# The gMLP layer's u and z as seven products of 2x2 blocks in place of eight

## The chip, the cores and the metric

One NeuronCore of a Trainium2 chip runs the whole step. The metric is the device time of one execution in microseconds. A NeuronCore has a matrix engine (TensorE, PE in the profile), a vector engine (VectorE, DVE), an engine for functions and copies (ScalarE, ACT), a general engine (GpSimd, POOL) and one whose instructions issue most DMAs (SyncE, SP). Each runs its own instruction stream in the order in which it was written, and semaphores join them.

## What is computed

The reference is one step of a model of two layers, over 512 prompt and 128 sample tokens (640 columns or five token tiles of 128). Layer 0 is a Mamba-2 mixer, which the change leaves as it was. Layer 1 is a gMLP:

```python
proj = h @ w_in                         # 1024 -> 3 x 2048
u = gelu(proj[..., :G_WIDTH])
v = gelu(proj[..., G_WIDTH:2 * G_WIDTH])
z = proj[..., 2 * G_WIDTH:]
v = layer_norm(v, ln_w, ln_b)
s = W_s @ v + b                         # 128x128 position matrix per group, 8 groups
y = u * s * silu(z)
out = y @ w_out                         # 2048 -> 1024, added to the residual
```

and a last RMS norm follows. All of it is float32. Each float32 product is made of three passes in TensorE's reduced format: operands are split in a high part (a rounding cast) and a low part (what is left), and high x high, high x low and low x high are summed.

## The kernel before

`Stream` (lines 103 to 136) brings weight blocks of 128x1024 from DRAM, two blocks ahead; `wsplit` casts the high part on ACT (L99) and subtracts it on DVE (L100) for the low part. `mm` (L69) is every matrix product.

Layer 1 has three stages. **v**: `v_tile` makes four blocks `vb` of 512 features for five token tiles `t`, 24 products of 512 columns each. Through block 0, the transposes of the normed input (`hT`, high and low; ACT L230, DVE L231) for tile t+1 are put in the middle of tile t. The weights of the next block are cast while tile 4 of a block runs. A GELU (ACT L756) and statistics follow each tile, and in block 3 the normalization (DVE L763). The mixing matrices `spt` are loaded whole (L773), and their row sums `pr` (L736) made in this stage.

**u and z**: a loop over 16 feature tiles f (eight groups g, two tiles each). Per f, `in_proj` makes u and then z: 8 blocks of the input x 3 passes x two halves (384 and 256 columns), so 96 products. Five products with `spt` (`sp`, `sq`) mix the positions of v. GELU, tanh and DVE products give y, which `split` takes apart (ACT L294, DVE L295). The output projection of group g-1 (`out_proj`, 60 products of 512 columns, added to the residual by `accB`, DVE L801) stands between the two f of group g, for g from 1 to 6. In groups 0 to 3, POOL multiplies and adds a 256-column piece of v (L834, L835) for an output.

**The end**: behind f=15 the last two output projections stand one after the other; the last one's pieces go into `final`, the last norm.

PE's stream is in the written order. On the other engines a scheduler sets the order at build time, and it is then fixed.

Of the kernel before, what the change touches and what calls it, by code (L numbers as in the profile page):

```python
# [27 lines left out]
# columns of the packed small constants  # L28
_C = {}
_off = 0  # L30
for _n, _w in (("nw0", 8), ("ident", 128), ("dtb", 32), ("alog", 32), ("sel", 32), ("blk", 8),
               ("triP", 128), ("triS", 128), ("sufP", 128), ("sufS", 128),
               ("convw", 128), ("convb", 32), ("dskip", 16), ("anw", 16), ("lnw", 16), ("lnb", 16)):
    _C[_n] = (_off, _off + _w)
    _off += _w
NCST = _off
NCST1 = _C["triP"][0]      # loaded first
# [3 lines left out]
def hybrid_step(ctx: ExitStack, tc: tile.TileContext, xin, xT0, cst, wdt, cache, wA, wAo, h0in, wB, wBv, wBo,  # L41
# [4 lines left out]
    # ------------------------------------------------------------ shared pools  # L46
# [10 lines left out]
    csb = const.tile([P, NCST], F32, name="csb")  # L57
    ones = const.tile([P, P], F32, name="ones")
    V.memset(ones, 1.0)
    S.activation(small.tile([P, 1], F32, name="pre"), ones[:, 0:1], AF.Exp)      # loads the function table  # L60

    def C(n):
        a, b = _C[n]
        return csb[:, a:b]

    ident, triP, triS = C("ident"), C("triP"), C("triS")

    def mm(out, lhsT, rhs, start=True, stop=True):
        T.matmul(out, lhsT=lhsT, rhs=rhs, start=start, stop=stop)  # L69
# [36 lines left out]
    class Stream:  # L106
# [8 lines left out]
        # the first weights, in pieces  # L115
# [26 lines left out]
    # feature-major input times the norm weight, in H/L, and with it the projections to dt and to the first  # L142
    # feature tile; the norm's factor of each token (rs; on every partition: rb) is applied to the projections
    def norm_first(zp, rb):
        xH, xL = norm_tiles()
        xt = zp.tile([P, KD, NT], F32, name="xt")
        nc.sync.dma_start(out=csb[:, :8], in_=cst[:, :8])
# [7 lines left out]
        nc.sync.dma_start(out=csb[:, 8:NCST1], in_=cst[:, 8:NCST1])  # L155
# [12 lines left out]
        def dt_step(k):          # rows 0-31 with the high parts of the weights, rows 32-63 with the low ones  # L168
# [52 lines left out]
    # its transpose, feature-major, in H/L  # L221
# [11 lines left out]
    # feature tile of an input projection: W[:, tile].T @ x.T, in two column halves  # L233
# [8 lines left out]
    # column sums of [feature, token], tokens to partitions: [token, tile]  # L242
# [9 lines left out]
    side = deque()            # pieces of other work to put between the steps  # L252
# [16 lines left out]
    # token-major output projection of two feature tiles, added to h1  # L269
# [47 lines left out]
    for g in range(GROUPS):  # L317
        units += [(wB[f],) for f in (2 * g, 16 + 2 * g)]
        if 0 < g < GROUPS - 1:
            units += [(wBo[f],) for f in (2 * g - 2, 2 * g - 1)]  # L320
        units += [(wB[f],) for f in (2 * g + 1, 17 + 2 * g)]
    units += [(wBo[f],) for f in (12, 13, 14, 15)]
# [3 lines left out]
    # ============================================================ layer 0: SSD mixer  # L326
    with ExitStack() as ca:
# [5 lines left out]
        rb = ap.tile([P, NT], F32, name="rb")  # L333
        xT, px0, rs, norm_fin, norm_half = norm_first(pp, rb)
# [5 lines left out]
        nc.sync.dma_start(out=csb[:, NCST1:], in_=cst[:, NCST1:])  # L340

        cw = ap.tile([P, 160], F32, name="cw")        # half the conv weights and biases
        V.tensor_scalar(cw, csb[:, _C["convw"][0]:_C["convb"][1]], 0.5, None, ALU.mult)
# [3 lines left out]
        # ---------------- dt, decays (token-major [token, tile, head])  # L347
# [23 lines left out]
        # cumulative sums within each chunk (128 tokens of the prompt, 16 of a stream)  # L371
# [3 lines left out]
        # chunk totals, on every partition: 4 prompt chunks, then 8 streams  # L375
# [4 lines left out]
        # la and its exponential with heads on partitions, in DRAM, from where a head's row goes to all partitions  # L380
# [68 lines left out]
        for g in range(GROUPS):  # L449
# [14 lines left out]
            # x, B, C of the group; x and B also token-major  # L464
# [22 lines left out]
            # sample tokens in high and low parts; by way of DRAM, the parts of the 16 tokens of a stream come  # L487
            # one below the other, so that one pass gives all four products of a state's update
# [22 lines left out]
            # decays from each token to each later one of its chunk  # L511
# [45 lines left out]
            # ---- prompt states  # L557
# [16 lines left out]
            # ---- sample states, decayed, and what they give to y  # L574
# [18 lines left out]
            # ---- C B^T, masked  # L593
# [36 lines left out]
            # ---- y, by pairs of heads  # L630
# [30 lines left out]
            # ---- new sample states  # L661
# [11 lines left out]
            # ---- gate: g2 = 2 y silu(z); the factor 2 is taken back in the group norm  # L673
# [53 lines left out]
    # ============================================================ layer 1: gMLP mixer  # L727
    with ExitStack() as cb_:
        bp = cb_.enter_context(tc.tile_pool(name="bp", bufs=1))
        hT = hH, hL = norm_tiles()  # L730
        rsb = bp.tile([P, 8, 2, P], F32, name="rsb")

        # row sums of the mixing matrices, on every partition
        def row_sums(q, g4):
            pr = ps_m.tile([P, 4, P], F32, name="pr", tag="m")
            mm(pr, ones, spt[:, q, 4 * g4:4 * g4 + 4, :])  # L736
            S.copy(out=rsb[:, 4 * g4:4 * g4 + 4, q, :], in_=pr)

        # ---- v, token-major
        v = bp.tile([P, TT, 4, 512], F32, name="v", tag="v")  # L740
        st6 = bp.tile([P, TT, 4, 6], F32, name="st6")

        def v_tile(Wv, vb, t, mid=lambda: None):
            tsl = slice(t * P, (t + 1) * P)
            ps = bank("oomm"[(vb * TT + t) % 4], "pv")
            for k in range(KD):
# [7 lines left out]
                if t == 4 and k % 2:  # L754
                    stream.fill(k // 2 + 1)
# [9 lines left out]
        cv = ExitStack()  # L765
        rpool = cv.enter_context(tc.tile_pool(name="rpool", bufs=2))
        stream.pools.update({stream.n + i: rpool for i in range(16) if i % 4 > 1})
        with tc.tile_pool(name="xsp", bufs=1) as xsp:
# [3 lines left out]
            spt = bp.tile([P, 2, 8, P], F32, name="spt")     # prompt W^T, sample W^T  # L772
            nc.sync.dma_start(out=spt, in_=spc)  # L773
            bsb = bp.tile([P, 8, 2, P], F32, name="bsb")     # prompt b, sample b
            nc.sync.dma_start(out=bsb, in_=bsp)
# [176 lines left out]
```

## Time and profile before

| | us |
|---|---|
| median of 3 runs | 1116.09 |
| lowest, highest | 1112.14, 1117.57 |
| span of the profiled execution | 1111.9 |
| PE busy | 1057.9 (95%) |
| DVE busy | 786.4 (71%) |
| ACT busy | 393.7 (35%) |
| POOL busy | 212.0 (19%) |

The span is that of one execution under the profiler, from its first to its last instruction; it stands 0.24 us under the lowest run and 4.2 us under the median. Busy shares are means over all stages; layer 1's stages have to be read one by one.

### The profile page before, as it was taken

To read this page: it belongs to the slowest core of one execution; us is meant where nothing else is said; L and a number is where in the kernel's file an instruction comes from. 1 tells how busy PE (TensorE), PEld (TensorE's weight loads), DVE (VectorE), ACT (ScalarE), POOL (GpSimd) and SP (SyncE) were. 2 spreads that over 40 slices of the span, in tenths; PEclk is the share of its full clock that TensorE was granted. 3 is DMA by queue.
4 is the path that set the end of the run, shared out by engine and by line. 5 is a ranking of instruction groups with operands and counts; after the bars stand their busy time and mean duration, and the time that the engine had idled before them with its cause. 6 is when DMAs were issued, how large, how long until landed. Compare 5 with 4: busy or idle time off the path is not lost. (4 is left out here: it accounts for less than half of the span.)

```text
span 1111.9 us, 16826 instructions
## 1 busy us (share of the span) xinstructions
PE 1057.9 (95%) x6571; PEld 957.8 (86%) x6571; DVE 786.4 (71%) x1351; ACT 393.7 (35%) x691; POOL 212.0 (19%) x290
## 2 busy tenths in 40 slices
PE   8998999998998999989999999999999999999994
PEld 7897888798898897988997788889999999999983
DVE  7969887878879879798789942386545645545357
ACT  6363516226254162352542432222132122222214
POOL 3444322404214234052132000002200000000004
PEclk9898999999999999999999999999999999999997
DMA  7453435243362352523632522113332122221202
GB/s 250 138 182 113 162 94 174 83 157 121 95 206 85 98 179 89 187 85 94 206 97 97 224 76 76 48 59 122 109 101 76 57 85 69 76 74 54 82 19 95
DMA packets 50560, 124.89 MB, mean 112 GB/s; under 512 B 8593, under 2 KB 21137, under 8 KB 50225
## 3 DMA queue, kind: packets, MB, share of 16 engines
q1 hardware_dynamic: 50480, 123.81, 34.5%
q8 instruction: 52, 0.85, 0.3%
q14 instruction: 28, 0.22, 0.1%
HBM read 106.93 MB, written 16.86 MB: 111 GB/s over the span
## 5 line engine op out<-in xcount | busy, mean ns | idle before, releaser
L69 PE MATMUL pin<-xH,wh 128*128 128x256 f32 (+1 forms) x1280 | 409.3, 320 | 10.9 <-DVE xp L416 10.2
L69 PE MATMUL pin<-xH,wl 128*128 128x256 f32 (+1 forms) x1280 | 398.2, 311 | 0.5 <-DVE wl L100 0.5
L69 PE MATMUL pin<-xL,wh 128*128 128x256 f32 (+1 forms) x1280 | 398.2, 311 | 0.0
L69 PEld LDWEIGHTS pin<-xH,wh 128*128 128x128 f32 x1280 | 244.5, 191 | 19.6 <-ACT xc L432 11.2
L69 PEld LDWEIGHTS pin<-xL,wh 128*128 128x128 f32 x1280 | 245.0, 191 | 0.7 <-issue 0.3
L69 PEld LDWEIGHTS pin<-xH,wl 128*128 128x128 f32 x1280 | 244.6, 191 | 0.8 <-DVE wl L100 0.8
L99 ACT CAST wh<-raw 128x1024 fp32r<-128x1024 f32 x127 | 132.2, 1046 | 236.5 <-PE pin L69 127.2
L69 PE MATMUL pop<-wh,yHL 128*128 128x512 f32 x640 | 205.4, 402 | 5.8 <-DVE hs L570 5.1
L100 DVE TENSOR_TENSOR wl<-raw,wh 128x1024 fp32r<-128x1024 f32 x104 | 130.3, 1257 | 64.3 <-ACT wh L99 63.0
L69 PEld LDWEIGHTS pop<-wh,yHL 128*128 128x128 f32 x640 | 117.3, 188 | 36.4 <-DVE hs L570 7.8
L426 DVE SCALAR_TENSOR_TENSOR acc<-xp,cw,acc 128x664 f32<-128x664 f32 x96 | 114.4, 1192 | 17.9 <-ACT acc L423 16.6
L69 PE MATMUL pop<-wl,yHL 128*128 128x512 f32 x320 | 126.4, 395 | 0.0
L69 PEld LDWEIGHTS pop<-wl,yHL 128*128 128x128 f32 x320 | 60.1, 188 | 14.3
L801 DVE SCALAR_TENSOR_TENSOR h<-pop,h 128x512 f32<-128x512 f32 x80 | 53.7, 687 | 25.1 <-PE pop L69 24.2
L690 DVE SCALAR_TENSOR_TENSOR h<-pop,rr,h 128x512 f32<-128x512 f32 x80 | 59.0, 745 | 13.3 <-PE pop L69 13.2
L849 POOL TENSOR_TENSOR h<-h,fnw_sb 128x512 f32<-128x512 f32 x10 | 12.9, 1285 | 287.1 <-ACT oo L848 286.7
L69 PE MATMUL pv<-wh,xH 128*128 128x512 f32 x160 | 63.5, 397 | 0.0
L69 PE MATMUL pv<-wh,xL 128*128 128x512 f32 x160 | 62.4, 390 | 0.4 <-DVE xL L231 0.4
L69 PE MATMUL pv<-wl,xH 128*128 128x512 f32 x160 | 62.3, 389 | 0.0
L100 POOL TENSOR_TENSOR wl<-raw,wh 128x1024 fp32r<-128x1024 f32 x23 | 56.0, 2437 | 12.3 <-ACT wh L99 12.3
L519 ACT ACTIVATE E<-E,la 128x128 f32<-128x128 f32 x160 | 51.5, 390 | 17.1 <-DMA E<-laD 17.1
L432 ACT ACTIVATE xc<-acc 128x512 f32<-128x512 f32 x64 | 26.6, 463 | 71.2 <-DVE acc L426 71.2
(176 smaller groups left out, 1234.0 us busy)
## 6 DMA issues: line engine op xcount, KB each, us to landing
raw<-wA SPq DMA_DIRECT2D x47, 512.0 KB, 3.8
raw<-wB SPq DMA_DIRECT2D x32, 512.0 KB, 3.6
E<-laD SPq DMA_DIRECT2D x32, 320.0 KB, 6.4
h<-h0in SPq DMA_DIRECT2D x16, 512.0 KB, 4.5
raw<-wAo SPq DMA_DIRECT2D x16, 512.0 KB, 3.8
out_sspS<-h SPq DMA_DIRECT2D x16, 512.0 KB, 3.8
raw<-wBv SPq DMA_DIRECT2D x16, 512.0 KB, 4.6
raw<-wBo SPq DMA_DIRECT2D x16, 512.0 KB, 3.9
```

What stands on the lines that cost most here:

```text
L69: T.matmul(out, lhsT=lhsT, rhs=rhs, start=start, stop=stop)
L99: S.copy(out=H, in_=raw)
L100: eng.tensor_tensor(out=L, in0=raw, in1=H.bitcast(F32), op=ALU.subtract)
L426: V.scalar_tensor_tensor(acc[:, 0:664], xp[:, k:k + 664], cw[:, 4 * ft + k:4 * ft + k + 1], acc[:, 0:664], ALU.mult, ALU.add)
L432: S.activation(o, a, AF.Tanh)
L519: S.activation(E_[:, t, :], E_[:, t, :], AF.Relu, bias=la[:, t, h:h + 1], scale=-1.0)
L690: V.scalar_tensor_tensor(h1[:, t, dsl], ps, rg[:, t:t + 1], h1[:, t, dsl], ALU.mult, ALU.add)
L801: V.scalar_tensor_tensor(h1[:, t, dsl], ps, 0.5, h1[:, t, dsl], ALU.mult, ALU.add)
L849: G.tensor_tensor(out=h1[:, t, dsl], in0=h1[:, t, dsl], in1=fnw_sb[:, dsl], op=ALU.mult)
```

## The change

u and z of one feature tile are seen as a 2x2 block product: the rows of the left matrix are u's and z's weights, its columns the two halves of the 1024 input features (blocks a11, a12, a21, a22 of 128x512), and the right matrix's blocks are the input's feature halves x token halves of 320 columns. Seven products m1 to m7 of summed blocks, in Winograd's form of Strassen's scheme, take the place of the eight.

- `Forms` loads u's and z's raw block, adds and subtracts 512-column pieces on POOL (L758, L760, L761, L765), and splits each of seven pieces (ACT L744, DVE L745). Pieces of the output weights go the same way, unsummed.
- The input's summed blocks are made once, from high and low parts, in ten POOL instructions of 1280 columns written into block 1 of v (`t1_`, `t2_`, `t34_`; L848, L851); each sum is split (ACT L854, DVE L855) into `tf`, the fourth (t3) over block (0,1) of the input after the last tile of v.
- `prod` is 12 products of 320 columns; seven of them make 84 per f. PSUM sums of products are joined by ACT copies (L953, L958), DVE adds (L955, L963, L965, L974) and one POOL add (L959).
- `position` loads the mixing matrices per group, in a pool that takes over the space of the summing stage; `pr`, of 256 columns, opens each group.
- The output projection of group g-1 stands before the second f in every group from 1 to 7. Behind the loop only the last one is left.

```diff
+        def split(self, src):
+            t = wpool.tile([P, 2, 512], F32R, name="wf", tag="wh" if len(self.got) % 2 == 0 else "wl", bufs=4)
+            S.copy(out=t[:, 0], in_=src)
+            V.tensor_tensor(out=t[:, 1], in0=src, in1=t[:, 0].bitcast(F32), op=ALU.subtract)
+            self.got.append(t)
...
+            def first():
+                G.tensor_tensor(out=t1, in0=a21, in1=a22, op=ALU.add)
+                self.split(a11)
+                G.tensor_tensor(out=a21, in0=a11, in1=a21, op=ALU.subtract)
+                G.tensor_tensor(out=a11, in0=t1, in1=a11, op=ALU.subtract)
+            def a12_():
+                self.split(a12)
+                G.tensor_tensor(out=a12, in0=a12, in1=a11, op=ALU.subtract)
+            return [first, lambda: self.split(a11), lambda: self.split(t1), a12_, lambda: self.split(a21),
+                    lambda: self.split(a12), lambda: self.split(a22)]
...
+            def t1_():
+                sub(ta, f12[0], f11[0])
+                sub(tx, f12[1], f11[1])
+                add(ta, ta, tx)
+                hilo(ta, tf[:, 0, 0], tf[:, 0, 1])
...
+                    if vb == 1 and t in (0, 2, 4):
+                        (t1_, t2_, t34_)[t // 2]()
+            hilo(t3, *block(0, 1))
...
+        def position(g):
+            spt = wk.tile([P, 2, P], F32, name="spt", tag="spt", bufs=2)
+            nc.sync.dma_start(out=spt, in_=spc[:, :, g, :])
+            G.memset(spt[64:128, 0, 0:64], 0.0)
...
-                if i and 0 < g < GROUPS - 1:
-                    out_proj([stream.next(), stream.next()], prev, accB, banks="oommoommoo")
+                if i and g:
+                    Ws = out_weights()
+                    for p in range(2 * TT):
+                        out_piece(Ws, prev, p)
...
+                prod(pa, "m1", True)
+                S.copy(out=c1, in_=pa)
+                prod(pb, "m6", True)
+                V.tensor_tensor(out=uu[:, hi], in0=pb, in1=c1, op=ALU.add)
+                pc = ps_m.tile([P, 512], F32, name="pqc", tag="m")[:, :HT]
+                prod(pc, "m5", True)
+                S.copy(out=c5, in_=pc)
+                G.tensor_tensor(out=c5, in0=c1, in1=c5, op=ALU.add)
+                prod(pa, "m2", False)
+                S.activation(uu[:, lo], pa, AF.Gelu)
+                prod(pb, "m7", False)
+                V.tensor_tensor(out=zz[:, hi], in0=pb, in1=c5, op=ALU.add)
+                prod(pc, "m3", False)
...
+                prod(pb, "m4", False)
+                V.tensor_tensor(out=zz[:, lo], in0=pb, in1=c1, op=ALU.add)
```

Three places in the instruction order. The first is ACT where block 1 of v begins (`v<-pv` is a GELU, `wh` a weight cast, `tf` the cast of a summed input block). Before:

```order
L756 ACTIVATE v_6395<-pv_6647 128x512
L99 CAST wh_6697<-raw_6695 128x1024
L99 CAST wh_6709<-raw_6707 128x1024
L99 CAST wh_6721<-raw_6719 128x1024
L99 CAST wh_6733<-raw_6731 128x1024
L756 ACTIVATE v_6395<-pv_6688 128x512
L756 ACTIVATE v_6395<-pv_6740 128x512
```

After:

```order
L819 ACTIVATE v_6395<-pv_6632 128x512
L99 CAST wh_6682<-raw_6680 128x1024
L854 CAST tf_6397<-tx0_6728 128x1280
L99 CAST wh_6694<-raw_6692 128x1024
L99 CAST wh_6706<-raw_6704 128x1024
L854 CAST tf_6397<-tx1_6729 128x1280
L99 CAST wh_6718<-raw_6716 128x1024
L819 ACTIVATE v_6395<-pv_6673 128x512
L854 CAST tf_6397<-tx0_6728 128x1280
L819 ACTIVATE v_6395<-pv_6732 128x512
```

and POOL there, which had no instruction at this place before:

```order
L848 TENSOR_TENSOR tx0_6728<-xH_6393 128x1280
L848 TENSOR_TENSOR tx3_6731<-xL_6394 128x1280
L848 TENSOR_TENSOR tx2_6730<-xH_6393 128x1280
L851 TENSOR_TENSOR tx0_6728<-tx0_6728,tx3_6731 128x1280
L848 TENSOR_TENSOR tx1_6729<-xH_6393,tx0_6728 128x1280
L848 TENSOR_TENSOR tx3_6731<-xL_6394 128x1280
L851 TENSOR_TENSOR tx1_6729<-tx1_6729,xL_6394 128x1280
L851 TENSOR_TENSOR tx2_6730<-tx2_6730,tx3_6731 128x1280
L848 TENSOR_TENSOR tx0_6728<-xH_6393,tx1_6729 128x1280
L851 TENSOR_TENSOR tx0_6728<-tx0_6728,xL_6394 128x1280
```

The casts of block 1's weights now have casts of summed inputs between them, the first behind POOL's fourth instruction and the second behind its seventh.

The second is PE at the end of v (`pv`), before:

```order
L69 MATMUL pv_7244<-wh_7058,xL_6393 128x512
L69 MATMUL pv_7244<-wl_7059,xH_6392 128x512
L69 MATMUL pin_7318<-xH_6392,wh_7253 128x384
L69 MATMUL pin_7318<-xL_6393,wh_7253 128x384
L69 MATMUL pin_7318<-xH_6392,wl_7254 128x384
```

After:

```order
L69 MATMUL pv_7246<-wh_7060,xL_6394 128x512
L69 MATMUL pv_7246<-wl_7061,xH_6393 128x512
L69 MATMUL pr_7343<-spt_7338,ones_83 128x256
L69 MATMUL pqa_7354<-xH_6393,wf_7259 128x320
L69 MATMUL pqa_7354<-xL_6394,wf_7259 128x320
```

and DVE there (`wf` is a split of a weight piece; the row of `xL` makes the low part of t3):

```order
L745 TENSOR_TENSOR wf_7289<-raw_7253,wf_7289 128x512
L745 TENSOR_TENSOR wf_7298<-raw_7255,wf_7298 128x512
L745 TENSOR_TENSOR wf_7307<-raw_7301,wf_7307 128x512
L820 BN_STATS st6_6396<-v_6395 128x6
L855 TENSOR_TENSOR xL_6394<-tx2_6730,xH_6393 128x4x320
```

The first product of the u and z stage was one with streamed weights; now it is `pr`, whose `spt` is loaded into space that the summing stage gives up with DVE's `xL<-tx2`.

The third is PE behind the last f. Before:

```order
L69 MATMUL sp_10073<-spt_6417,v_6395 128x128 x4
L69 MATMUL sq_10074<-spt_6417,v_6395 128x128
L69 MATMUL pop_10103<-wh_9955,yHL_9583 128x512 x2
L69 MATMUL pop_10103<-wl_9956,yHL_9583 128x512
L69 MATMUL pop_10103<-wh_10014,yHL_9812 128x512 x2
```

After:

```order
L69 MATMUL sp_10461<-spt_9701,v_6395 128x128 x4
L69 MATMUL sq_10462<-spt_9701,v_6395 128x128
L69 MATMUL pqb_10351<-tf_6397,wf_10391 128x320 x12
L69 MATMUL pop_10500<-wf_10412,yHL_10248 128x512 x3
L69 MATMUL pop_10500<-wf_10444,yHL_10494 128x512 x3
L69 MATMUL pop_10510<-wf_10428,yHL_10248 128x512 x3
L69 MATMUL pop_10510<-wf_10468,yHL_10494 128x512 x3
```

Before, the last but one output projection (60 products on group 6's y) follows `sq`, and the first product on the last f's y is the 64th behind it; now it is the fourth behind the last `m4` (`yHL_10494` is the last f's y).

## Rows read from the trace of the kernel before

**Rows 1.** Stages of layer 1 (windows): length, then busy us by engine, PEclk, DMA.
```profile
658.00:742.50 84.50, 84.50 (x371) 69.07 (x370) 38.38 (x80) 22.12 (x29) 0.00 (x0) 1.00 0.20 66
742.50:1070.60 328.10, 328.10 (x2061) 311.64 (x2060) 171.81 (x249) 83.01 (x126) 15.08 (x16) 1.00 0.26 83
1070.60:1111.90 41.30, 27.26 (x117) 21.60 (x115) 30.61 (x72) 14.03 (x30) 12.85 (x10) 0.87 0.17 64
```

**Rows 2.** Chain of waits, pieces in order of time: start us, us, what.
```profile
742.64 14.09 PE pin L69 x96
...
788.26 13.99 PE pop L69 x60
...
1069.87 18.20 PE pop L69 x78
```

**Rows 3.** Timeline of PE where v ends: start us, us, instruction.
```profile
742.25 0.39 PE L69 MATMUL pv<-wl,xH 128*128 128x512 f32 x1
742.48 0.33 PE L69 MATMUL pin<-xH,wh 128*128 128x384 f32 x1
```

**Rows 4.** Lines by form, PE: busy us, mean ns, idle before.
```profile
L69 PE MATMUL pr<-spt,ones 128*128 128x512 f32 x8 | 3.9, 592 | 0.0
```

**Rows 5.** Timeline of ACT around the second block of v.
```profile
650.57 1.08 ACT L230 CAST xH<-pt 128x512 fp32r<-128x512 f32 x2 [2.56 <-PE pt L228]
...
654.89 1.06 ACT L99 CAST wh<-raw 128x1024 fp32r<-128x1024 f32 x1 [0.54 <-PE pv L69]
```

**Rows 6.** Timeline of PE, first tile of the second block of v.
```profile
659.00 0.39 PE L69 MATMUL pv<-wh,xH 128*128 128x512 f32 x1
...
663.53 0.39 PE L69 MATMUL pv<-wl,xH 128*128 128x512 f32 x1
```

**Rows 7.** Lines by form, POOL.
```profile
L100 POOL TENSOR_TENSOR wl<-raw,wh 128x1024 fp32r<-128x1024 f32 x23 | 56.0, 2437 | 12.3 <-ACT wh L99 12.3
...
L849 POOL TENSOR_TENSOR h<-h,fnw_sb 128x512 f32<-128x512 f32 x10 | 12.9, 1285 | 287.1 <-ACT oo L848 286.7
```

**Rows 8.** Lines by form, ACT and DVE: the weight split.
```profile
L99 ACT CAST wh<-raw 128x1024 fp32r<-128x1024 f32 x127 | 132.2, 1046 | 236.5 <-PE pin L69 127.2 <-PE pop L69 85.2 <-DMA raw<-wA 6.4
...
L100 DVE TENSOR_TENSOR wl<-raw,wh 128x1024 fp32r<-128x1024 f32 x104 | 130.3, 1257 | 64.3 <-ACT wh L99 63.0
```

**Rows 9.** Timelines of POOL, then of DVE: additions and splits, side by side and alone.
```profile
758.78 0.74 POOL L834 TENSOR_TENSOR lwb<-v,lwb 128x256 f32<-128x256 f32 x1 [6.09 <-DMA lwb<-lnwb]
759.60 1.20 POOL L835 TENSOR_TENSOR lwb<-lwb 128x256 f32<-128x256 f32 x1
...
760.12 1.75 DVE L100 TENSOR_TENSOR wl<-raw,wh 128x1024 fp32r<-128x1024 f32 x1
...
1071.67 1.22 DVE L100 TENSOR_TENSOR wl<-raw,wh 128x1024 fp32r<-128x1024 f32 x1
```

**Rows 10.** Windows around PE's longest wait (2.9 us).
```profile
100.00:104.00 4.00, 2.74 (x11) 2.23 (x11) 3.84 (x9) 3.69 (x8) 0.40 (x2) 0.59 0.38 125
104.00:108.00 4.00, 4.00 (x28) 3.44 (x28) 3.02 (x3) 0.94 (x2) 2.35 (x1) 0.56 0.53 165
```

**Rows 11.** DMA issues: count, KB each, median us to landing.
```profile
out_sspP<-hs SPq DMA_DIRECT2D x8, 128.0 KB, 1.7
...
dw<-wdt SPq DMA_DIRECT2D x1, 128.0 KB, 3.0
```

**Rows 12.** Timelines of DVE, then of ACT, behind the last mixing product.
```profile
1070.35 0.41 DVE L816 SCALAR_TENSOR_TENSOR thb<-thb,pin 128x256 f32<-128x256 f32 x1
...
1070.94 0.82 DVE L817 TENSOR_TENSOR uu<-uu,thb 128x640 f32<-128x640 f32 x1
...
1072.81 0.82 DVE L838 TENSOR_TENSOR uu<-uu,sb 128x640 f32<-128x640 f32 x1
...
1074.74 0.82 DVE L295 TENSOR_TENSOR yHL<-uu,yHL 128x640 fp32r<-128x640 f32 x1
...
1073.71 0.73 ACT L294 CAST yHL<-uu 128x640 fp32r<-128x640 f32 x1 [3.72 <-DVE uu L838]
```

More of the change, by code (lines that the diff above doesn't have):

```diff
@@ L725, in hybrid_step, with __init__, raw, start @@
     out_proj([stream.next(), stream.next()], *pend.pop(GROUPS - 1))
+    class Forms:
+        def __init__(self, items, pool):
+            self.items, self.pool, self.got, self.n = items, pool, [], 0
+        def raw(self, src, i):
+            r = (self.pool if i else wpool).tile([P, 1024], F32, name="raw", tag="raw", bufs=2)
+            nc.sync.dma_start(out=r, in_=src)
+            return r
+        def split(self, src):
[3 more added lines that the diff above has]
+            self.got.append(t)
+        def start(self):
+            kind, s0, s1 = self.items.pop(0)
+            r0, r1 = self.raw(s0, 0), self.raw(s1, 1)
+            a11, a12, a21, a22 = r0[:, :512], r0[:, 512:], r1[:, :512], r1[:, 512:]
+            if kind == "o":
+                return [lambda x=x: self.split(x) for x in (a11, a12, a21, a22)]
+            t1 = self.pool.tile([P, 512], F32, name="s1", tag="s1", bufs=1)
+            def first():
[8 more added lines that the diff above has]
+                    lambda: self.split(a12), lambda: self.split(a22)]
+        todo = []
+        def fill(self, ahead):
+            while len(self.got) < self.n + ahead and (self.items or self.todo):
+                if not self.todo:
+                    self.todo = self.start()
+                self.todo.pop(0)()
+        def next(self, ahead):
+            self.fill(1 + ahead)
+            r = self.got[self.n]
+            self.got[self.n] = None
+            self.n += 1
+            return r[:, 0], r[:, 1]
     with ExitStack() as cb_:
@@ L730, in hybrid_step, with block @@
         hT = hH, hL = norm_tiles()
[L731 to L737, printed above, removed]
+        HT = NT // 2
+        def block(k, j):
+            ks, js = slice(4 * k, 4 * k + 4), slice(HT * j, HT * j + HT)
+            return hH[:, ks, js], hL[:, ks, js]
         v = bp.tile([P, TT, 4, 512], F32, name="v", tag="v")
         st6 = bp.tile([P, TT, 4, 6], F32, name="st6")
+        forms = Forms([x for g in range(GROUPS) for x in
+                       [("q", wB[2 * g], wB[16 + 2 * g])]
+                       + ([("o", wBo[2 * g - 2], wBo[2 * g - 1])] if g else [])
+                       + [("q", wB[2 * g + 1], wB[17 + 2 * g])]]
+                      + [("o", wBo[14], wBo[15])], bp)
         def v_tile(Wv, vb, t, mid=lambda: None):
@@ new lines, in hybrid_step, with prod @@
+        wk = cb_.enter_context(tc.tile_pool(name="wkb", bufs=2))
+        X = dict(m1=block(0, 0), m2=block(1, 0), m3=block(1, 1), m7=block(0, 1))
+        X |= {m: (tf[:, i, 0], tf[:, i, 1]) for i, m in enumerate(("m5", "m6", "m4"))}
+        def prod(ps, m, start, ahead=4):
+            wH, wL = forms.next(ahead)
+            xH, xL = X[m]
+            for k in range(4):
+                ks = slice(k * P, (k + 1) * P)
+                mm(ps, wH[:, ks], xH[:, k], start=(start and k == 0), stop=False, skip_group_check=not start)
+                mm(ps, wH[:, ks], xL[:, k], start=False, stop=False, skip_group_check=not start)
+                mm(ps, wL[:, ks], xH[:, k], start=False, stop=(k == 3), skip_group_check=not start)
@@ L800, in accB, with out_weights, out_piece @@
         def accB(ps, t, dsl):
             V.scalar_tensor_tensor(h1[:, t, dsl], ps, 0.5, h1[:, t, dsl], ALU.mult, ALU.add)
+        def out_weights():
+            w = [forms.next(3) for _ in range(4)]
+            return w[:2], w[2:]
+        def out_piece(Ws, ys, p, after=None):
+            t, dh = p // 2, p % 2
+            tsl, dsl = slice(t * P, (t + 1) * P), slice(dh * 512, (dh + 1) * 512)
+            ps = bank("oommoommoo"[p], "pop")
+            for i in range(2):
+                (wH, wL), (yH, yL) = Ws[i][dh], ys[i]
+                mm(ps, yH[:, tsl], wH, start=(i == 0), stop=False)
+                mm(ps, yL[:, tsl], wH, start=False, stop=False)
+                mm(ps, yH[:, tsl], wL, start=False, stop=(i == 1))
+            accB(ps, t, dsl)
+            if after is not None:
+                after(t, dsl, dh)
```

133 lines of the change are left out of this document (79 added, 54 removed).

## Prediction

> **What bounds the kernel now.** I read the stages of layer 1 first [rows 1]. In the u and z stage (742.5 to 1070.6 us) PE is busy for all of 328.1 us at full clock, while DVE works 171.8, ACT 83.0 and POOL 15.1 us of it: only fewer product columns shorten this stage, and there is room on the other engines on average. In v (658 to 742.5) PE is busy throughout and POOL does nothing. The last stage is mixed: PE 27.26 of 41.3 us. The chain of waits then shows what the stage is made of [rows 2]: per feature tile f one piece of 96 products in 14.09 us, and 13.99 us per output projection; the last piece, 78 products in 18.20 us, shows that the chain behind the last f is hidden under the last but one output projection. Last I look at where stages meet: the last product of v starts at 742.25 and the first of u at 742.48 [rows 3], no gap.
>
> **Part 1, the products.** The halves of 384 and 256 columns have a mean of 320, which is the new width, so 14.09 us / 96 = 0.1468 us is the price of a product of 320 columns by the mean of its two neighbours. Per f 84 products take the place of 96, an eighth less: 14.09 / 8 = 1.76 us, by 16 f **-28.2 us**. Output projections and mixing products stay. `pr` had eight products of 512 columns, 3.9 us [rows 4], and gets the same columns in eight of 256 and twice the places: 0.
>
> **Part 2, the input sums, at block 1 of v.** PE comes to this block at 659.00 and to the product that needs the low part of the fourth weight block at 663.53 [rows 6]. The four weight casts began at 654.89 [rows 5]. Now two casts of sums stand between them on ACT, and wait for POOL. POOL's first subtraction can start when the first half of the last token tile is cast, 650.57 + 0.54 = about 651.1 [rows 5]. Its price: 1285 ns for 512 columns and 2437 for 1024 [rows 7] make 1152 per 512, so 1280 columns are 2437 + 576 = 3.01 us. The first sum is ready after four of them (663.2), the second after seven (672.2). ACT: the cast of a sum is 1046 x 1280/1024 = 1.3 us at most [rows 8]; the second ends at 673.5, and the fourth weight cast, queued behind it, at 674.5. DVE: low part of the sum 1257 x 1.25 = 1.6 us [rows 8], to 675.1, then the weight's, 1.26: 676.3. So PE stands 676.3 - 663.5 = **12.8 us** if nothing else slows POOL.
> But it will be slowed. Where a POOL addition and a DVE split lie side by side, POOL's goes from 0.74 to 1.20 us and DVE's from 1.22 to 1.75 [rows 9]. About 5.4 us of such DVE work lies beside POOL before the second sum (three weights, 3.8, and one sum, 1.6), and 0.46 us per 1.22 of it makes 2.0 us; the two DVE steps at the end, 2.9 us, stretch by up to 0.53/1.22, 1.2 us. Sum 16.0: I take **+16**, with ends 12.8 (no meeting) and 20 (the stretch twice as large).
> The Trainium skill says, in "GPSIMD Engine Reference", Key points, that POOL shares its SBUF interfaces with DVE and contends with DVE instructions that have two SBUF inputs, and that elementwise work is about twice as fast on DVE. The two rows bear it out; without such sharing this term would be 12.8 and my sum 3.2 us lower, and the rule speaks against the ten additions' place.
> Then the clock. Around a wait of 2.9 us the granted clock was 0.59 and 0.56 in two windows of 4 us [rows 10], between the levels 2.4 and 1.2 GHz; of full speed that loses 0.41 x 2.74 + 0.44 x 4.00 = 2.9 us, of which part can lie in the wait. I take **+2** for this wait, ends 0 and 3.
>
> **Part 3, where v ends.** PE's first instruction is now `pr`; it waits for POOL's memset of `spt`, that for the load, and that for DVE's low part of t3, which frees the space. Count from T, the end of v. Weight pieces wait for slots that v's last products free, so POOL's sum for the next f, its a21 and this f's a12 (three of 1.285 us [rows 7], the first begun some 1.4 us ahead of T) end at T+2.5. Behind them ACT casts three pieces of about 0.57 us (half of 1046 and a little) and a GELU of 0.6: T+4.8. DVE is then at the last pieces' low parts and statistics (0.7 each), T+6.2, and does t3's low part, 1.6: about T+7.7. The load of 128 KB lands in 1.7 to 3.0 us [rows 11]: T+9.4 to T+10.7. I take **+10.5** for PE's wait, ends 8.5 (no split late) and 13 (POOL and DVE stretched as in part 2), and for the clock behind it again **+2**, ends 0 and 3. Behind `pr` the weights' pieces are ready.
>
> **Part 4, the end.** Behind the last `m4` come an add of 320 columns (about 0.48, between 0.41 for 256 columns and the 0.82 of 640), tanh (0.73 by the cast of the same width), four DVE steps at 0.82 and one cast of 0.73 [rows 12]: 0.48 + 0.73 + 3.28 + 0.73 = 5.2 us, with handovers 5.6. Only three products of 512 columns (0.23 each [rows 3]) stand between: **+4.9**, ends 3.5 (some hidden) and 7 (weight splits queued between on DVE). The clock behind it: +0.5, ends 0 and 1.5, since DVE sets the pace of the last norm anyway. The output projection that was the cover (13.99) is only moved to an earlier place.
>
> **Part 5, u and z otherwise.** Per f, DVE gets seven half splits for two whole ones (4.4 for 2.5 us), four adds of about 0.48 and a whole-width step for two halves (0.82 for 0.97): +3.6 us, by 16 58, so 230 of 300 us. POOL gets four additions of 1.285 and one of about 0.9: 6.0 us per f. What covers it is that pieces are made four ahead; handovers: **+2**, ends 0 and 6. The loads of `spt` go out one group ahead; a group's some 40 us of products hide their 3 us, and without that cover each of seven would cost what part 3 has.
>
> **Sum**: -28.2 + 16 + 2 + 10.5 + 2 + 4.9 + 0.5 + 2 = **+9.7 us**. The sum stands on the profiled execution, 1111.9 us of span, 0.24 under the lowest run; the median is 1116.09, 4.2 above that span. Put on the median: **1125.8 us**. Ends of all terms together: -3.4 and +25.3.
>
> **Rivals.**
> *No held casts* (faster). If POOL's first seven instructions were done before PE needs the casts (some 659, so 1.1 us each), part 2 falls away: 9.7 - 18 = -8.3, 1107.8 us. For it speaks only that no row shows 1280 columns on POOL; against it the two sizes that rows 7 show. If ACT could pass a waiting cast it would come out the same way. The Trainium skill ("TensorE: Matmul & The Clock Gate", Engine queue depths) says ACT and DVE queues are strictly in order; no row here shows an ACT instruction passing another. Chance 0.13.
> *Early mixing matrices* (no change). If t3's low part is done beside v's last products, `spt` lands as v ends and part 3 falls away: 9.7 - 12.5 = -2.8, 1113.3 us. Against it: t3 is written over a block that v's last products still read. Chance 0.12.
> *DVE becomes the bound* (slower still). POOL's new 6.0 us per f are 96 us; if each stretched DVE by as much as itself, DVE would have 230 + 96 = 326 us in a stage of 300: +26 less the 2 above, 1149 us; it decides from 70/96 = 0.73 us of stretch per us of POOL on. Rows 9 give 0.53 us for an addition of 0.74 alone, 0.72, if every one of them met a split of two inputs from SBUF; DVE's reads from PSUM are among the rest, and they do not all meet. Chance 0.10.
> That seven products would not be seven is excluded by the instruction order: 84 per f.
>
> **How the numbers follow.** About 0.5% (5.6 us) is what a measurement of this kernel can tell from no change. My forecast has 0.65; its own range, with some terms at their low and others at their high ends, is 1113 to 1141, and 0.14 of the 0.65 lies under 1121.7 (0.13 within 0.5%, 0.01 below that). With the rivals: faster by over 0.5% 0.13 + 0.01 = 0.14 (no held casts), within 0.5% 0.12 + 0.13 = 0.25 (early matrices), slower 0.51 + 0.10 = 0.61. For the range: from 1106, under which the lower half of the first rival lies, to 1140, past which lie most of the third rival and the forecast's extreme; this leaves out 0.2.
>
> **What would show it.** In the profile after: piece lengths of 12 products near 1.76 us and u and z without output projections at 13.2 us per f (part 1); PE waiting 13 to 20 us in the first tile of block 1 of v, for DVE's split of a weight block, with ACT's idle time before a `tf` cast released by POOL (part 2); PE waiting 8 to 13 us for the memset ahead of the first `pr` (part 3); about 5 us of PE idle before the fourth `pop` of the end (part 4); granted clock under 0.8 behind the first two waits. If PE runs through block 1 or through the start of u and z without a wait, I am wrong; if DVE is busy throughout u and z with PE waiting for `wf` at each f, the third rival holds.

## The result and the profile after

| | before | after |
|---|---|---|
| median, us | 1115.37 (4 runs) | 1144.02 (1140.09 to 1146.56, 4 runs) |
| span of the profiled execution | 1111.9 | 1140.8 |
| ratio after to before | | 1.0262, 95% interval 1.0231 to 1.0292 |

The changed kernel is 2.6% slower. The forecast, slower and 1125.8 us, had the sign and the places; its size and its range (to 1140) were too small. I read the stages first, since the 28.9 us between the spans of the two profiled executions can be divided there.

In the steady part the products gain what was forecast. Here is one whole group (two f and an output projection, from the start of one output projection to the start of the next), first of before, then of after (length, then busy us of PE, PEld, DVE, ACT, POOL; granted clock, DMA share, GB/s):

```profile
921.20:965.60 44.40, 44.40 (x275) 41.68 (x274) 22.61 (x32) 10.66 (x17) 0.00 (x0) 1.00 0.23 72
912.00:953.30 41.30, 41.30 (x252) 38.42 (x251) 34.44 (x51) 16.89 (x32) 13.76 (x11) 1.00 0.27 84
```

That is 41.3 us for 44.4, PE busy throughout at full clock: 3.1 us less, where 2 x 1.76 less 0.24 for `pr` had been due. The other groups of after, from the third on, take up to 41.5, so the gain is 2.9 to 3.1. Eight groups are worth some 25 us. All else is loss, and the view of what PE waits for (us in total, times, longest) names it:

```profile
PE pr L69 <- POOL spt L923: 14.4, 1, 14.4
PE pv L69 <- DVE wl L100: 10.6, 3, 5.0
...
PE pv L69 <- ACT wh L99: 5.6, 1, 5.6
...
PE pop L69 <- ACT yHL L294: 4.1, 1, 4.1
...
PE pqb L69 <- DVE uu L955: 1.6, 1, 1.6
```

- **Block 1 of v** (`pv`): 5.6 + 10.6 us. The product that needs the fourth weight's low part was due 4.53 us behind the tile's first [rows 6], at 664.4, and ran at 684.66: 20.3 us late, with the slow clock between the waits.
- **End of v** (`pr`, for POOL's memset of `spt`): 14.4 us, then slow clock.
- **The last y** (`pop` for ACT's `yHL`): 4.1 us.

By stretches: from the cast of the last token tile to the end of v 112.7 us (before 92.1, with 1.9 us for four products of `pr` in it, which are no longer there): +20.6. The wait for `pr`: +14.4. From the first product of u and z to the first output product behind the last f took 326.8 us with seven output projections, before 327.1 with six; a projection is 14.0, so -14.3, not -25: 10.5 us are lost, nearly all of them up to the second output projection (870.5 us). From there to the end 35.4 us, before 42.3 with a projection, 28.3 without: +7.1. Layer 0 ended 0.9 us later. The sum is 28.7 us of the 28.9.

The clock behind the first wait, in the same windows view; [rows 10] showed two such windows of before:

```profile
665.00:670.00 5.00, 1.22 (x2) 0.50 (x2) 4.01 (x2) 2.85 (x3) 5.00 (x2) 0.53 0.00 0
...
680.00:685.00 5.00, 0.34 (x1) 0.34 (x2) 5.00 (x3) 0.00 (x0) 4.92 (x2) 0.50 0.00 0
685.00:690.00 5.00, 5.00 (x14) 3.90 (x14) 1.51 (x2) 1.76 (x2) 2.38 (x1) 0.58 0.34 105
690.00:695.00 5.00, 5.00 (x24) 4.14 (x23) 1.50 (x3) 0.60 (x1) 0.00 (x0) 1.00 0.00 0
```

PE ran at the lower of its two levels (granted 0.50 to 0.53) through the waits and got 0.58 of full clock in the 5 us behind them: 0.42 x 5 = 2.1 us lost, as forecast (2).

Now the same place on DVE and POOL (timelines: start us, us, instruction, and the idle time before it):

```profile
652.08 2.95 POOL L848 TENSOR_TENSOR tx<-xH 128x1280 f32<-128x1280 f32 x1 [60.18 <-ACT xH L230]
655.00 2.95 POOL L848 TENSOR_TENSOR tx<-xL 128x1280 f32<-128x1280 f32 x1
...
667.60 4.13 POOL L848 TENSOR_TENSOR tx<-xL 128x1280 f32<-128x1280 f32 x1
671.70 3.89 POOL L851 TENSOR_TENSOR tx<-tx,xL 128x1280 f32<-128x1280 f32 x1
675.54 3.90 POOL L851 TENSOR_TENSOR tx<-tx,tx 128x1280 f32<-128x1280 f32 x1
679.41 4.13 POOL L848 TENSOR_TENSOR tx<-xH,tx 128x1280 f32<-128x1280 f32 x1
```

And DVE in the same stretch, its splits of weights (`wl`) and of an input sum (`tf`):

```profile
668.92 7.74 DVE L100 TENSOR_TENSOR wl<-raw,wh 128x1024 fp32r<-128x1024 f32 x2
676.91 3.89 DVE L855 TENSOR_TENSOR tf<-tx,tf 128x1280 fp32r<-128x1280 f32 x1 [0.24 <-ACT tf L854]
680.72 3.89 DVE L100 TENSOR_TENSOR wl<-raw,wh 128x1024 fp32r<-128x1024 f32 x1
```

POOL's 1280 columns take 2.95 us alone, 3.9 to 4.1 beside such a DVE step: [rows 7] had given 3.01 and [rows 9] some more, so the second sum came at 675.6, where the forecast gave 674.2 (0.8 us of it is that block 1 began later). But DVE's weight split, 1.26 us [rows 8], takes **3.87 to 3.89 us** here, as long as POOL's instruction beside it. The forecast had let the two steps behind the second sum stretch by 1.2 us in all; they stretched by 4.9 (3.89 + 3.89 for 2.9).

The ends of these rows tell why. POOL's instructions end at 675.59, 679.44 and 683.54 us, DVE's steps at 676.66, 680.80 and 684.61: a split of 1024 columns ends 1.07 us behind POOL's instruction and the one of 1280 columns 1.36, not much less than each takes alone, and POOL's next instruction ends 2.7 to 2.8 us behind the DVE step. So in these rows the two do not run slowly side by side, they take turns: each waits for the other's whole instruction and then takes its own time.

The timeline of DVE at the end of v:

```profile
760.59 0.15 DVE L80 TENSOR_SCALAR rr<-rx 128x1 int32<-128x1 int32 x1
...
761.46 1.34 DVE L88 SCALAR_TENSOR_TENSOR rt<-rr,rx 128x1 f32<-128x1 f32 x1
...
766.19 1.21 DVE L89 SCALAR_TENSOR_TENSOR rr<-rt,rr 128x1 f32<-128x1 f32 x1
...
767.93 2.85 DVE L826 TENSOR_SCALAR v<-v,mv,rr 128x512 f32<-128x512 f32 x4
...
773.11 2.22 DVE L855 TENSOR_TENSOR xL<-tx,xH 128x1280 fp32r<-128x1280 f32 x1
```

And SP's queue, where the load of `spt` waits for the last of these:

```profile
775.40 0.62 SPq L922 DMA_DIRECT2D spt<-spc  x1
```

Some of the small steps of the norm, 0.16 to 0.22 us alone, take 1.2 to 1.3 where POOL adds beside them, the norm of a tile 2.85 for 1.92, and the low part of t3 2.22 for 1.49. That chain ends at 775.3, 11.2 us behind the end of v, for 7.7 forecast; the load takes 2.75 more, the memset ends it.

From 775 to 824 us the chain of work that ended last (start us, us, what) does not run through PE at all:

```profile
777.96 3.26 DMA lwb<-lnwb
...
782.95 1.88 DMA out_vs<-lwb
...
784.89 2.90 DMA lwb<-lnwb
...
788.40 0.70 POOL lwb L989
789.10 1.71 POOL raw L760
790.80 1.29 POOL c L959
```

These are the loads and stores of the 256-column pieces of v (`lwb`): one buffer, so load, two POOL steps and store follow each other, and POOL's weight additions and `c` stand in one queue with them. The forecast has no cost for `lwb`, whose instructions were there before; but before, nothing that PE needs stood behind them on POOL.

### The profile page after: what moved, and what is told of

The parts are those of the page before. It is cut to its first block, busy times and chain, and to the rows that moved or that the text cites. A ratio compares the mean times of both kernels' runs of the same rounds, so it can differ in the third digit from the quotient of the medians.

```text
span 1140.8 us, 17021 instructions
## 1 busy us (share of the span) xinstructions
PE 1048.2 (92%) x6387; PEld 942.2 (83%) x6387; DVE 902.9 (79%) x1499; ACT 444.1 (39%) x811; POOL 357.7 (31%) x387
## 5 line engine op out<-in xcount | busy, mean ns | idle before, releaser
L69 PE MATMUL pin<-xH,wh 128*128 128x384 f32 (+1 forms) x768 | 251.5, 328 | 10.8 <-DVE xp L412 10.1
L69 PE MATMUL pin<-xL,wh 128*128 128x384 f32 (+1 forms) x768 | 241.5, 314 | 0.0
L69 PE MATMUL pin<-xH,wl 128*128 128x384 f32 (+1 forms) x768 | 240.9, 314 | 0.0
L69 PEld LDWEIGHTS pin<-xH,wh 128*128 128x128 f32 x768 | 148.5, 193 | 19.1 <-ACT xc L428 11.2
L69 PEld LDWEIGHTS pin<-xL,wh 128*128 128x128 f32 x768 | 148.8, 194 | 0.4 <-issue 0.3
L69 PEld LDWEIGHTS pin<-xH,wl 128*128 128x128 f32 x768 | 148.7, 194 | 0.0
L745 DVE TENSOR_TENSOR wf<-raw,wf 128x512 fp32r<-128x512 f32 x128 | 107.5, 851 | 39.1 <-ACT wf L744 39.1
L69 PE MATMUL pop<-wf,yHL 128*128 128x512 f32 x480 | 117.6, 403 | 5.5 <-ACT yHL L294 4.1
L744 ACT CAST wf<-raw 128x512 fp32r<-128x512 f32 x128 | 78.7, 619 | 102.7 <-POOL raw L761 33.6
L69 PEld LDWEIGHTS pop<-wf,yHL 128*128 128x128 f32 x480 | 90.7, 192 | 30.1 <-ACT yHL L294 4.5
L69 PE MATMUL pop<-wh,yHL 128*128 128x512 f32 x320 | 104.3, 407 | 5.7 <-DVE hs L566 5.0
L100 DVE TENSOR_TENSOR wl<-raw,wh 128x1024 fp32r<-128x1024 f32 x56 | 78.4, 1403 | 10.7 <-ACT wh L99 9.7
L69 PE MATMUL pv<-wl,xH 128*128 128x512 f32 x160 | 64.7, 405 | 10.6 <-DVE wl L100 10.6
L69 PE MATMUL pqa<-xH,wf 128*128 128x320 f32 x256 | 64.4, 321 | 0.0
```

What stands on the lines that cost most here:

```text
L69: T.matmul(out, lhsT=lhsT, rhs=rhs, start=start, stop=stop, **kw)
L100: eng.tensor_tensor(out=L, in0=raw, in1=H.bitcast(F32), op=ALU.subtract)
L744: S.copy(out=t[:, 0], in_=src)
L745: V.tensor_tensor(out=t[:, 1], in0=src, in1=t[:, 0].bitcast(F32), op=ALU.subtract)
```

## The experiments

All are built on the changed kernel, or on earlier ones as said; ratios are to the kernel before. Layer 0 ended up to 7.6 us apart from one profiled execution to the next, so layer 1 is compared beside the medians: from the last cast of its normed input (ACT L230, 650.57 us in [rows 5]) to the end it took 461.3 us before and 489.4 in the changed kernel.

### The additions away from the weight casts

```diff
+            def gate(t, vb):
+                G.tensor_tensor(out=t[:, 0, 0:2], in0=st6[:, 0, vb, 0:2], in1=st6[:, 0, vb, 2:4], op=ALU.add)
             def t1_():
+                gate(ta, 1)
+                gate(tx, 1)
...
             def t34_():
+                gate(ta, 2)
+                gate(t3, 2)
+                gate(tx, 2)
...
-                    if vb == 1 and t in (0, 2, 4):
+                    if (vb, t) in ((1, 0), (1, 1), (2, 0)):
```

> Edit: the ten input additions are held back by a two-column POOL addition that reads the statistics of the first tile of block 1 of v (first five) and of block 2 (last five), so that they lie behind the weight casts and splits, not among them. Theory (the casts wait for POOL and the splits share with it): the first tile of block 1 runs through, v ends 20 us earlier than in the changed kernel, time 1122 to 1127 us. Rival (the additions slow the splits of the next block instead): v ends only 5 to 12 us earlier, time 1132 to 1139.

Measured: 1119.82 us, ratio 1.0049 (1.0024 to 1.0075), 24 us less by the medians; layer 1 took 466.2 us, 23 less, and v 91.4. What PE waits for in this kernel, the two big waits and the one left in v:

```profile
PE pr L69 <- POOL spt L931: 14.4, 1, 14.4
...
PE pop L69 <- ACT yHL L294: 4.1, 1, 4.1
...
PE pv L69 <- DVE wl L100: 0.9, 1, 0.9
```

One wait of 0.9 us is left of 16.2, and the other two big ones stand as they were. The ten additions still take POOL 31.8 us (35.4 in the changed kernel); what changed is what lies beside and behind them. The theory holds, 2 us under the low end that it gave.

### Order and sharing apart

Here POOL adds as early as in the changed kernel, but ACT's casts of sums come behind the weight casts (held by a two-column DVE step):

```diff
-            def hilo(t, H, L):
+            def hilo(t, H, L, late=True):
+                if late:
+                    V.tensor_tensor(out=H[:, 0, 0:2], in0=st6[:, 0, 1, 0:2], in1=st6[:, 0, 1, 2:4], op=ALU.add)
                 S.copy(out=H, in_=t)
...
-            hilo(t3, *block(0, 1))
+            hilo(t3, *block(0, 1), False)
```

> Edit, on the changed kernel alone: a two-column DVE addition from the statistics of the first tile of block 1 writes into the place of each input sum's high part first, so that the casts of sums come behind the four weight casts; POOL's ten additions stay where they are. It parts the two causes of the wait in that tile (20.3 us there). Theory (both count: ACT's order, and the weight splits on DVE that take 3.9 us instead of 1.25 beside POOL): the splits end 2.2 + 3 x 3.9 us from 656.8, at 670.7, for a need at 664.4, so the wait falls to 5 to 8 us, time 1128 to 1133. Rival (order alone): under 2 us, time 1123 to 1126. Rival (sharing alone): over 15 us.

Measured: 1128.47 us, ratio 1.0140 (1.0103 to 1.0177); v is 14 us shorter than in the changed kernel. PE's wait in v there (us in total, times, longest):

```profile
PE pv L69 <- DVE wl L100: 5.5, 3, 2.2
```

And the timelines of DVE, then of POOL:

```profile
658.12 13.83 DVE L100 TENSOR_TENSOR wl<-raw,wh 128x1024 fp32r<-128x1024 f32 x4 [0.90 <-ACT wh L99]
...
675.47 5.07 DVE L855 TENSOR_TENSOR tf<-st 128x2 fp32r<-128x2 f32 x3
...
674.68 2.92 POOL L851 TENSOR_TENSOR tx<-tx,xL 128x1280 f32<-128x1280 f32 x1
677.56 2.96 POOL L851 TENSOR_TENSOR tx<-tx,tx 128x1280 f32<-128x1280 f32 x1
```

The four splits take 13.83 us beside POOL's additions, where one takes 1.26 otherwise [rows 8], and PE waits 5.5 us: that is what is left with sharing and without the order. The other 10.7 of the 16.2 us of waiting came with the order, the casts behind sums that were not yet there. Both causes count, as the first theory had it. DVE's last row is a by-product: three additions of **two columns** take 5.07 us beside POOL. Taken singly, the first two last 2.15 and 2.93 us and end at 677.62 and 680.54, within 0.02 us of the ends of POOL's two additions; the third adds nothing to the sum. So such a step costs what is left of the POOL instruction that it meets, whatever its own length.

### A place of its own for the mixing matrix

```diff
-            spt = wk.tile([P, 2, P], F32, name="spt", tag="spt", bufs=2)
+            spt = bp.tile([P, 2, P], F32, name="spt", tag="spt", bufs=2)
```

(and `bsb` likewise, with `position(0)` ahead of the summing stage).

> Edit: the mixing matrix and bias of a group get a place of their own for the whole layer, so that the first load does not wait for space. Theory (the first product waits for that space alone): the product starts with the end of v, the wait of 14.4 us falls away and 3 us of low clock with it, less a wait of about 4 us for the input's low part at the fifth of the seven products: 10 to 14 us less, 1130 to 1134. Rival (the weight pieces and the low part of t3 are as late as the matrix, all behind the same DVE queue): at most 5 us less, 1139 to 1144.

Measured: 1144.64 us, ratio 1.0263 (1.0217 to 1.0310): nothing gained; the rival holds. Layer 1 took 488.8 us for 489.4. `pr` now follows v without a wait, but the time to the first product behind the first output projection is within 1 us as long as in the changed kernel (768.3 to 846.1, 77.8 us; there 14.4 of waiting and 64.4). PE's waits there:

```profile
PE pqc L69 <- ACT v L819: 3.3, 1, 3.3
PE pop L69 <- DVE uu L965: 3.3, 1, 3.3
...
PE pop L69 <- DVE h L910: 2.9, 1, 2.9
PE pqb L69 <- DVE zz L963: 2.6, 2, 2.1
...
PE pqa L69 <- ACT c L953: 1.5, 1, 1.5
```

In place of one long wait there are nine short ones, 16.2 us in all, six of them for DVE. So the wait for space, which I had named and priced, was where it happened and not what it cost: DVE and POOL were behind by that time whatever PE did.

### The cover at the end

```diff
-                if i and g:
+                if i and 0 < g < GROUPS - 1:
...
+        Ws = out_weights()
+        for p in range(2 * TT):
+            out_piece(Ws, prev2, p)
```

> Edit: the last but one output projection goes back behind the last feature tile, as in the kernel before. Theory (the chain of the last y lay open for want of cover): PE's wait of 4.1 us before the fourth product of the end falls away with the slow clock behind it, 5 to 7 us less, 1137 to 1139. Rival (the last norm's chain on DVE sets the end, PE's wait is beside it): under 2 us less.

Measured: 1138.12 us, ratio 1.0200 (1.0152 to 1.0247), 5.9 us less by the medians, hardly clear of the noise of four runs; but layer 1 took 482.7 us, 6.7 less, and the wait of 4.1 us is gone from PE's list. The theory holds.

### The three together

> Edit: the three edits together. Theory (three waits in a row, independent): the three gains add up, 35 to 41 us less than the changed kernel, 1103 to 1109, which is below the kernel before. Rival (DVE's total load is the limit and a wait removed returns at the next place): less than two thirds of the three single gains.

Measured: 1115.91 us, ratio 1.0013 (0.9985 to 1.0041): 28.1 us less, no different from before (layer 1 took 461.5 us, before 461.3). The single gains (24.2, -0.6 and 5.9) add up to 29.5, within the noise of the 28.1, so no return of a wait elsewhere is seen; the expected sum was too high mainly by what the second did not bring. The loss that is left lies in one place: from the first product of u and z to the first one behind the first output projection 78.8 us (743.23 to 822.06), where before took 59.6 (742.48 to 802.09) for the same work. I call this "the stretch" from here on. The next four runs start from this kernel.

### What POOL's weight additions cost

All four additions per f are left out; the pieces are split unsummed, so u and z are not the reference's.

> Edit, on the three edits together: all weight additions on POOL left out (four per f), so that u and z are not the right sums; PE, ACT and DVE have the same work as before the edit. It prices POOL's weight additions with all that they slow. Theory (they slow DVE by about as much as they last, 0.9 us per us): the stretch falls to 62 to 66 us, DVE's busy time in u and z by 40 to 80 us. Rival (DVE's own load): the stretch stays over 72.

Measured: 1092.66 us in one run; the stretch is 58.2 us (740.70 to 798.87), 20.6 less and under the 62 to 66 of the theory. DVE's busy time in the whole kernel fell by 33 us only (892.6 to 859.8), under the 40 to 80 expected. Windows of the stretch, first with the additions, then without:

```profile
743.00:822.00 79.00, 64.34 (x348) 58.46 (x347) 64.17 (x95) 27.25 (x51) 39.21 (x33) 0.87 0.29 94
740.00:799.00 59.00, 56.77 (x351) 53.20 (x350) 50.31 (x95) 26.69 (x50) 16.14 (x16) 1.00 0.37 119
```

For the same 95 instructions DVE is busy 13.9 us less (64.17 to 50.31). So lengthened DVE steps are a large part of the price; the run does not tell how the rest divides between waits in POOL's queue and the slower clock (0.87). The small steps of the norm show the sharing cleanly. DVE's timeline in the kernel of the three edits, with the additions, and two rows of POOL there:

```profile
756.00 0.48 DVE L963 TENSOR_TENSOR uu<-pqb,c 128x320 f32<-128x320 f32 x1
756.39 0.14 DVE L81 TENSOR_SCALAR rr<-rr 128x1 int32<-128x1 int32 x1
...
757.24 1.25 DVE L88 SCALAR_TENSOR_TENSOR rt<-rr,rx 128x1 f32<-128x1 f32 x1
...
758.80 1.25 DVE L89 SCALAR_TENSOR_TENSOR rr<-rt,rr 128x1 f32<-128x1 f32 x1
...
756.72 1.75 POOL L758 TENSOR_TENSOR s<-raw 128x512 f32<-128x512 f32 x1
758.55 1.49 POOL L760 TENSOR_TENSOR raw<-raw 128x512 f32<-128x512 f32 x1
```

And without them, the same steps:

```profile
750.25 0.21 DVE L88 SCALAR_TENSOR_TENSOR rt<-rr,rx 128x1 f32<-128x1 f32 x1
...
750.98 0.14 DVE L89 SCALAR_TENSOR_TENSOR rr<-rt,rr 128x1 f32<-128x1 f32 x1
```

1.25 us against 0.21 and 0.14 for the same instructions on 128x1: with the additions they end at 758.49 and 760.05, within 0.02 us of the ends of POOL's rows. Two steps did not wait for the POOL addition that ran from 755.89 to 756.77: the one-input step at 756.39 kept its 0.14, and the sum at 756.00, with one input in PSUM, its 0.48.

### The pieces of v in their own time, and the first additions ahead

First (on the three edits): `lwb` takes turns with `sb` for one buffer and comes behind y, so each piece is loaded in its own f.

```diff
-                    lwb = wk.tile([P, 2, 256], F32, name="lwb", tag="lwb", bufs=1)
+                    lwb = wk.tile([P, TT, P], F32, name="lwb", tag="sb", bufs=1)  ...
```

> Edit, on the three edits together (1115.9 us, where the stretch from the first product of u and z to the first product behind the first output projection takes 78.8 us; the kernel before needs 59.6 for the same work): the 256-column pieces of v for an output take turns with sb for one buffer, so that each piece comes in its own f, behind y, and not as early as its load allows. Theory (POOL's weight additions stand in its queue behind pieces that wait 5 us for a load, and from there the wait reaches PE before the first output projection, 3.2 + 2.9 us): the stretch falls to 68 to 73 us, time 1106 to 1111. Rival (the stretch is DVE's load alone): within 2 us of 78.8.

Measured: 1111.05 us, ratio 0.9948 (0.9922 to 0.9974); the stretch is 70.7 us (743.84 to 814.50), and layer 1 took 456.1 us, 5.4 less than with the three edits. As expected, with the time at the upper end.

Second (on the three edits): the first f's sums go to two tiles of the summing stage during block 3 of v.

```diff
+            if self.early is not None:
+                t2, t3 = [self.early.tile([P, 512], F32, name=f"s{i}") for i in (2, 3)]
+                self.early = None
+                G.tensor_tensor(out=t1, in0=a21, in1=a22, op=ALU.add)
+                G.tensor_tensor(out=t2, in0=t1, in1=a11, op=ALU.subtract)
+                G.tensor_tensor(out=t3, in0=a12, in1=t2, op=ALU.subtract)
+                G.tensor_tensor(out=a21, in0=a11, in1=a21, op=ALU.subtract)
+                return [lambda x=x: self.split(x) for x in (a11, t2, t1, a12, a21, t3, a22)]
```

> Edit, on the three edits together: the four weight additions of the first f are written to places of their own during block 3 of v, where POOL is idle, so that they don't wait for the splits, and no additions for the second f are made ahead. Theory (at the end of v DVE and POOL meet, and tiny steps of the last norms of 0.15 to 0.22 us take 1.2): the stretch falls from 78.8 to 66 to 72 us, with no wait before the third and fifth product groups of the first f; time 1103 to 1110. Rival (norms and splits on DVE are too much without POOL): falls by under 4 us.

Measured: 1112.44 us, ratio 0.9965 (0.9943 to 0.9987); the stretch is 75.5 us, 3.3 less. That is the rival's figure (under 4), although the time fell by 3.5: the norms and splits on DVE remain, and now the mixing product waits 3.8 us for the last norm.

Both together:

> Edit: the last two together, on the three. Theory: both gains add up, the stretch is 58 to 64 us and the time 1094 to 1102, under the kernel before by 1 to 2%. Rival (DVE has no room left in the first group): no better than the better of the two.

Measured: 1107.20 us, ratio 0.9918 (0.9887 to 0.9948); stretch 67.4 us. That is 8.7 us less than the three edits, of 4.9 and 3.5 singly: the gains add up, but stretch and time both missed the ranges expected.

### The last norm

On the kernel of both:

```diff
+                    G.tensor_tensor(out=t1[:, 0:1], in0=self.rs, in1=self.rs, op=ALU.add)
                 G.tensor_tensor(out=t1, in0=a21, in1=a22, op=ALU.add)
```

(for the second f's first addition only; `rs` is the last tile's).

> Edit, on the best so far (1107.2 us; its stretch from the first product of u and z to the one behind the first output projection is 67.4 us): POOL's first addition for the second f waits for the last rsqrt of v's norm, by a one-column addition that reads it. Theory (the tiny steps of that norm run into POOL's additions, and the mixing product waits 5.25 us for the norm): that wait falls to under 2 us and the stretch to 62 to 65 us, 1102 to 1105. Rival (the second f's pieces are now late): the wait shows up at the second f's products, no gain.

Measured: 1105.94 us, ratio 0.9938 (0.9913 to 0.9962), not told apart from the one before. The wait at the mixing product (5.3 us) is gone, the stretch is 67.3 us: waits for the second f's sums (2.5 and 2.8 us for `zz`) took its place. The rival holds.

> Edit, on the one before: in the first f the mixing products come behind the last of the seven products. Theory (the wait for the last tile's norm gets one product more of cover): 1 to 2 us less than that one, 1100 to 1104. Rival (what is late is the chain of y, not the product): within 1 us of it.

Measured: 1104.48 us, ratio 0.9925 (0.9905 to 0.9945), stretch 64.7 us; by the medians 1.5 us less than the one before, by the intervals no different; neither theory nor rival is settled by the times. This kernel and the two before it are 0.6 to 0.8% under the kernel before, a small gain but clear of the noise; which of the three is best is not settled.

## Why the prediction was wrong

Of the 19.0 us between the forecast (+9.7) and the measured +28.7, 6.5 lie in the first groups of u and z (10.5 lost for 4 in parts 3 and 5), 4.4 in part 2, 3.9 in the wait of part 3, 1.7 in part 4, 1.5 in the gain of the products (24.8 in the groups and 1.9 of `pr` that left v, for 28.2) and 0.9 in layer 0, which the change leaves alone.

- **Part 1 held.** 12 products of 320 columns take 1.76 us, a steady group 2.9 to 3.1 us less than before.
- **Part 2: the mechanism was right, one term mis-sized.** Casts behind sums, sums behind POOL: 16 + 2 forecast, 20.3 + 2.1 measured. POOL's own price was right. What failed is "the two DVE steps at the end, 2.9 us, stretch by up to 0.53/1.22, 1.2 us": that is a ratio from a row in which POOL's instruction was short (0.74 us alone). Beside POOL instructions of 3 us the same split takes 3.9 us, three times its time, since it waits for the whole of POOL's: the two steps stretched by 4.9.
- **Part 3: the place was right, its price and its meaning not.** 10.5 forecast, 14.4 measured, because four DVE steps on the way took 3.7 us more than alone (two small steps and the scaling of a norm that the forecast's count left out, and t3's low part); and taking the wait away gained nothing, since DVE and POOL then held PE up in the first groups.
- **Part 4** gave 5.4 with its clock; the end lost 7.1, and giving back the cover returned 5.9 by the medians.
- **Part 5 is the step that failed**: "What covers it is that pieces are made four ahead; handovers: +2, ends 0 and 6". 10.5 us were lost against the steady group, some 3 of them the clock term of part 3 (granted 0.50 from 778.5 to 783.5 us and 0.87 in the next 5). The lead of four pieces does not exist when the stage begins: two were split when v ended, and POOL's queue held weight additions behind `lwb` pieces that waited for loads. `lwb` had no cost in the forecast because its instructions were old ones; what was new is who stands behind them. Giving them their own time brought 4.9 us, and without any weight additions the stretch of the first groups fell by 20.6. Parts 3 and 5 are one cost in two places: 24.9 us for the 14.5 forecast.
- **The range.** All upper ends together came to +25.3 and the measured change is +28.7, so the ends themselves were too low: part 5's 6 for about 7.5, part 3's 16 with its clock for about 17.4, and part 1 had no ends. Parts 2 and 3 both rested on [rows 9] for DVE beside POOL, so they were not independent: they rose together.
- **The rivals.** "No held casts" did not come: PE waited 5.6 us for a held weight cast. "DVE becomes the bound" was near the truth for the first groups and wrong for the stage: in a steady group DVE is busy 34.4 of 41.3 us and PE waits for nothing. "Early mixing matrices" was tried in another way, with a place of their own, and gained nothing.

The Trainium skill states in "GPSIMD Engine Reference", Key points, that POOL contends with DVE instructions that have two SBUF inputs or are in a 2-port perf mode. The traces agree on the first: a one-input step of the norm (0.14 us) keeps its time beside POOL and the two-input ones go to 1.2. The scaling of a tile, one tensor with two scalars per token, grew too, from 1.92 to 2.85; no run here shows whether it is of the second kind. That statement gives no size; in the runs here a DVE step waited for what was left of POOL's instruction.

What stays open: how the 6.5 us between the stretch of the last kernel (64.7) and that without the additions (58.2) divide between lengthened steps and waiting queues, and whether the additions would be cheaper on DVE; neither was tried.

## What to carry to other kernels

A step that is moved to an idle engine costs what it does to the queues it joins: list who stands behind it there, and whose instructions wait for its own, before calling it hidden. A gain in a steady loop has to be weighed against the loop's start, where no lead exists; that is where a new chain of preparation is paid in full. And a wait that names one cause should be removed in a test before it is believed: here taking away the largest single wait gained nothing, and giving an older, unchanged piece of work its own time did.

## What the runs showed of the hardware

- A POOL `tensor_tensor` of 128x1280 takes 2.95 us alone. A DVE split of 128x1024 that meets it takes 3.9 us for 1.26, and POOL's goes to 3.9 or more: they take turns by whole instructions, and each split ended 1.07 to 1.09 us behind the POOL instruction that it met.
- The length of the DVE instruction does not matter: two-column steps took 2.15 and 2.93 us beside such POOL additions, one-column steps beside additions of 512 columns 1.2 (0.14 to 0.22 alone), and all of these ended within 0.02 us of POOL's instruction. In the rsqrt of the norm, a chain of such small steps, each can pay this anew.
- Two DVE steps did not wait for POOL: a one-input step of one column (0.14 us) and an addition with one input in PSUM (0.48 us).
- The same ten POOL additions, moved behind the weight splits, cost 24 us less.
